# Encoder layer: the weight-block sums issued in the first group's middle phase, the down projection's residual by tiles, one of its steps later

## The chip, the cores and the metric

The kernel runs on one core of one Trainium2 chip. The metric is the device time of one execution in microseconds, as the median of several runs. A core has TensorE (PE, matmuls into PSUM), VectorE (DVE), ScalarE (ACT), GpSimd (POOL) and SyncE (SP), whose queue issues nearly all DMAs here. Each engine runs its own queue of instructions in order. PSUM holds matmul results, SBUF holds tiles, DRAM the inputs, outputs and scratch tensors.

## The reference

One layer of an encoder, run on two request groups of 1024 tokens by 1024 channels with the same weights, in fp32:

```
proj = x @ w_in                                     # mixers A and B side by side
oa   = rmsnorm(dilated window attention(qa, ka, va))
ob   = rmsnorm(grouped-query attention(qb, kb, vb))
x    = LN1(alpha*x + [oa, ob] @ w_o)
x    = LN2(alpha*x + softmax(x wc_q (mem wc_k)^T / 16) (mem wc_v) wc_o)   # 256 memory tokens, 4 heads
u    = x @ w_up;  gate, val = halves of u           # 2816 columns each
x    = LN3(alpha*x + (gelu(conv3(gate)) * val) @ w_down)
```

alpha is 2^(1/4), LN is a layer norm with gain and bias, conv3 a depthwise convolution of width 3 over the tokens.

## The kernel before, in words

The two groups (g = 0, 1) go through the same phases one after the other: phase_in (projection), attention, phase_mid (output projection, cross attention, two layer norms), ffn_up and ffn_down; cross_prep, for both groups at once, stands between phase_in and attention of g = 0. Every fp32 operand is split into a high half, rounded to the form that TensorE takes at full rate, and a low half (the rest), and each product is three matmuls: high by high, high by low, low by high. ACT or POOL makes the high half, DVE or POOL the low half (L115, L126).

phase_mid's output projection takes w_o in two column halves n. For each half four weight blocks are loaded into `raw` buffers and split into `wts` tiles (wload, L269), and the eight row tiles ct of 128 tokens follow. The cross attention does the same with the products G of queries and keys (L965 to L985) and U of values and output weights (L987 to L1017), which cross_prep made. In its last loop each row tile is standardized into a `raw` buffer, stored to yD, and transposed later by x2t.

Both FFN projections are done by a scheme with seven products in place of eight (Winograd's form of Strassen's): sums and differences of blocks of both operands, with the products added up in PSUM and in the sums behind it. ffn_up goes over 22 column blocks f. up_sums (L1023) loads two blocks of w_up into `raw` and lets POOL make three sums of them; up_weights (L1042) splits seven weight tiles; prod (L1091) multiplies; DVE adds the products up (L1105 to L1115), which frees PSUM banks; end (L1117) does the convolution, GELU and the product with val for the block before. For each pair of blocks, end makes the three sums of the activations (s1, s2, s4) and stores blocks and sums to hD and hS in DRAM.

down_sums (L1194) makes the matching sums of w_down: for each j of 11 it loads two row blocks of w_down into two `raw` buffers, lets POOL make four differences in place (L1203, L1204, L1206, L1207) and stores both buffers to wD in DRAM. It is called in ffn_up of g = 0 alone, after product 5 of each odd f (L1172); both groups' ffn_down read wD.

ffn_down does seven products m (in the order SEVEN, L1182), each over 11 steps k, on 128-row blocks: 77 steps of 12 matmuls. d_in (L1210) loads what a step needs, one activation block and one weight block, and splits them: ACT copies the high halves (L109), POOL and DVE subtract one half each (L1233). The first five steps are loaded alone into `raw`, the others by pairs into `wts`. Its calls run up to seven steps ahead of the matmuls. Step k = 10 reads hD[10], which the last end stores. y, the residual, is read from yD with two loads of 2 MB (L1243) into the two `res` buffers that hold ffn_up's working tiles; it is multiplied by LN2's gain and its bias is added (L1298, L1299), for tiles 0 to 3 in steps 2 to 5 of the first product and for tiles 4 to 7 in steps 2 to 5 of the second. evac (L1260) adds a product from PSUM to y, finish (L1272) does the last layer norm and stores the output.

The order on each engine is made by a planner at build time: it walks the program, takes the instruction that its own estimates call ready, earlier program text first, and hands out buffers as they fall free in its plan. An instruction written late can so be issued early. issue_after gives the planner an order without a wait on the chip. `raw` is one pool of three buffers of 4 KB a partition for the whole kernel; `wts` has six.

```
                    if i == 5 and g == 0 and f % 2:        # ffn_up, L1172
                        self.down_sums(f // 2, wD)
                if m < 2 and 2 <= k < 6:           # ffn_down, L1295
                    v = yt(4 * m + k - 2)
                    nc.vector.tensor_mul(v, v, gb[0])
                    nc.vector.tensor_add(v, v, gb[1])
```

Of the kernel before, what the change touches and what calls it, by code (L numbers as in the profile page):

```python
# [18 lines left out]
NT = 8  # L19
NMEM = 256  # L20
DFF = 2816
NFF = DFF // 128
# [49 lines left out]
class Trunk:  # L72
# [760 lines left out]
        nc.scalar.activation(out, y, AF.Identity, bias=rs[:, 1:2], scale=rs[:, 0:1])  # L833


    def phase_mid(self, g, S, o2s, ob, G, U, yD):
        nc, a = self.nc, self.a
        es = ExitStack()
        P = lambda name, bufs=1: es.enter_context(
# [7 lines left out]
        self.dma(gain, bcast_rows(a["out_norm_b"], 512))  # L847
        gb = self.ln_load(1)
        mT = []

        def m_t(ct):
            if ct >= NT - 2:
# [13 lines left out]
        for n in range(2):  # L866
            ns = slice(n * 512, n * 512 + 512)
            w = self.wload(lambda kp: w_o[:, 2 * kp:2 * kp + 2, ns], fast=0, after=self.sp_last)
            for ct in range(NT):
                xr = wtile("xr")  # L870
                nc.sync.dma_start(xr, x[ct * 128:(ct + 1) * 128, ns])
                if len(mT) < NT:
                    m_t(len(mT))
                p = self.pB()
                self.gemm(p, mT[ct], w)
                nc.vector.scalar_tensor_tensor(yt(ct)[:, ns], xr, ALPHA, p, op0=ALU.mult, op1=ALU.add)
                if n == 1:
# [87 lines left out]
        for n in range(2):  # L965
            w = self.wload(lambda kp: G[g][n, 2 * kp:2 * kp + 2].rearrange("k p c -> p k c"), fast=1)
            for ct in range(NT):
                if ct % 2 == 0:
                    pp = self.at_slot(2 + 4 * n + ct // 2, [128, 2, 2, 4, 128])
                    pT[n] += [pp[:, 0], pp[:, 1]]  # L970
                p = self.pB()
                self.gemm(p, x1T[ct], w)
                mn = self.small.tile([128, 2], F32, name="cmn")
                nc.vector.tensor_reduce(mn, p.rearrange("p (h k) -> p h k", h=2), axis=X, op=ALU.min)
                s = wtile()
                den = self.small.tile([128, 2], F32, name="cden")
# [18 lines left out]
        for n, ct in [(n, ct) for j in range(NT // 2) for n in range(2) for ct in (2 * j, 2 * j + 1)]:  # L995
            if n == 0:
                st[ct] = self.small.tile([128, 2, 6], F32, name="bst")
            if (n, ct) == (0, NT - 2):
                self.up_sums0()
            ns = slice(n * 512, n * 512 + 512)  # L1000
            p = self.pB()
            for k in range(8):
# [57 lines left out]
    def ffn_up(self, g, B, todo, hD, hS, wD):  # L1060
# [56 lines left out]
        def end(e, f):  # L1117
# [9 lines left out]
            if f % 2:  # L1127
# [2 lines left out]
                j, (d0, d1) = f // 2, ds  # L1130
                ds.clear()
                a11, a21, a12, a22 = d0[:, :512], d0[:, 512:], d1[:, :512], d1[:, 512:]
                s1, s2, s4 = sets[1][:, 3584:], sets[0][:, 3584:], e.u3
                nc.gpsimd.tensor_add(s1, a21, a22)
                nc.sync.dma_start(hD[j, 1], d1)
                nc.gpsimd.tensor_sub(a21, a11, a21)
# [15 lines left out]
        for f in range(NFF):  # L1152
            e = begin(f)
# [11 lines left out]
            else:  # L1165
                for i in ORDER:
# [2 lines left out]
                        end(*last)  # L1169
                    if i == 5 and f < NFF - 1:  # L1170
                        ready.append(weights(f + 1))
                    if i == 5 and g == 0 and f % 2:  # L1172
                        self.down_sums(f // 2, wD)
                    if f == NFF - 1 and i in (7, 5, 2, 4, 3):
                        self.d_in(g)
            last = (e, f)
# [8 lines left out]
    def down_src(self, hD, hS, wD):  # L1185
# [2 lines left out]
        hv, sv, tv = [t.rearrange("j i p c -> p j i c") for t in (hD, hS, wD)]  # L1188
        self.hsrc = {1: hv[:, :, 0, l], 2: hv[:, :, 1, l], 6: sv[:, :, 1], 5: sv[:, :, 0],
                     7: hv[:, :, 0, r], 3: sv[:, :, 2], 4: hv[:, :, 1, r]}  # L1190
        self.wsrc = {1: w[:, :, 0, l], 2: w[:, :, 1, l], 6: tv[:, :, 1, r], 5: tv[:, :, 0, l],
                     7: tv[:, :, 0, r], 3: w[:, :, 1, r], 4: tv[:, :, 1, l]}

    def down_sums(self, j, wD):  # L1194

        nc = self.nc
        r = []
        for o in range(2):
            t = self.raw.tile([128, D], F32, name="raw")
# [10 lines left out]
    def d_in(self, g):  # L1210

        nc = self.nc
        s = len(self.ds)
        m, k = divmod(s, self.NK)
        i = self.SEVEN[m]
        if not self.dr:

            n = 1 if s < 5 else min(2, self.NK - k)
            if s < 5:
                r = self.raw.tile([128, 1, 2, 512], F32, name="raw")  # L1220
            else:
# [14 lines left out]
    def ffn_down(self, g, yD, out):  # L1236
# [2 lines left out]
        self.lnp = es.enter_context(self.tc.tile_pool(name="lnp", bufs=1, side="right", reuse_waits="tile"))  # L1239
        gb = self.ln_load(2)  # L1240
        y = [self.resid.tile([128, 4, D], F32, name="res") for _ in range(2)]
        for i in range(2):
            nc.sync.dma_start(y[i], yD[4 * i:4 * i + 4].rearrange("c p d -> p c d"))  # L1243
        yt = lambda ct: y[ct // 4][:, ct % 4]
        pa = [self.pA() for _ in range(2)]
        sets = [[p[:, n * 512:n * 512 + 512] for p in pa for n in range(2)],
                [self.pT(), self.pO(), self.pT(), self.pO()]]
# [2 lines left out]
                3: (0, 1, False), 4: (1, 0, True)}  # L1250
        stats = {}

        def mm(p, m, k, q):
            i, t = self.SEVEN[m], self.ds[m * self.NK + k]
            c = slice(q * 128, q * 128 + 128)
            for x, l in ((0, 0), (0, 1), (1, 0)):
                nc.tensor.matmul(p, t[:, x, 0, c], t[:, l, 1], start=i in (1, 2, 5) and k + x + l == 0,  # L1257
                                 stop=k == self.NK - 1 and x == 1, skip_group_check=True)

        def evac(i, q, p):  # L1260
            th, n, first = goal[i]
# [14 lines left out]
        for m, i in enumerate(self.SEVEN):  # L1276
            bank = sets[m % 2]
            if i == 4:
                gb = self.ln_load(3)
                if g:  # L1280

                    while len(self.ds) < 7 * self.NK:
                        self.d_in(g)
                    for q in range(4):
                        for k in range(self.NK):
                            mm(bank[q], m, k, q)
                        finish(q)
                        evac(i, q, bank[q])
                        finish(4 + q)
                    break  # L1290
            for k in range(self.NK):
                s = m * self.NK + k
                while len(self.ds) < min(s + 7, 7 * self.NK):
                    self.d_in(g)
                if m < 2 and 2 <= k < 6:  # L1295

                    v = yt(4 * m + k - 2)
                    nc.vector.tensor_mul(v, v, gb[0])  # L1298
                    nc.vector.tensor_add(v, v, gb[1])  # L1299
                if i == 4 and k % 2 and k < 8:  # L1300
                    finish(k // 2)
                for q in range(4):
                    mm(bank[q], m, k, q)
# [8 lines left out]
    def run(self, stages=None):  # L1312
# [9 lines left out]
        for g in range(2):  # L1322
# [28 lines left out]
            with ExitStack() as es:  # L1351
                gemm_pools(es, 14)
                if "mid" in stages:
                    yD = dt(f"yD{g}", [NT, 128, D])
                    hD, hS = dt(f"hD{g}", [NFF // 2, 2, 128, T]), dt(f"hS{g}", [NFF // 2, 3, 128, 512])
                    B, todo = self.phase_mid(g, S, o2s, ob, G, U, yD)
# [43 lines left out]
```

## Time and profile before

| | us |
|---|---|
| median of 3 runs | 3297.7 (3297.68 to 3300.06) |
| the profiled execution, its own time | 3297.42 |
| its span, first to last instruction | 3295.6 |
| TensorE busy | 3124.1 (95%) |
| VectorE busy | 1929.7 (59%) |
| GpSimd busy | 1831.7 (56%) |
| ScalarE busy | 1325.8 (40%) |

The mean granted clock of TensorE is 0.973 of its 2.4 GHz. DMA moved 426.66 MB, a mean of 129 GB/s. A share of the span is an average over phases with different limits, so the rows further down are taken by phase. In order of time the phases of g = 0 end at about 217 us (phase_in), 405 (cross_prep), 735 (attention), 1030 (phase_mid), 1530 (ffn_up) and 1767 (ffn_down); those of g = 1 at about 1985, 2312, 2607, 3044 and 3295.

### The profile page before, as it was taken

Reading aid. Unit: us, or ns where it says so; the run is one execution under the profiler, and the core shown is the slowest. Engines: PE = TensorE matmul, PEld = TensorE weight load, DVE = VectorE, ACT = ScalarE, POOL = GpSimd, SP = SyncE. Lnnn points to the kernel's source line nnn. Section 1 sums busy time; section 2 is a strip of 40 time slices with the busy share of each in tenths; the row PEclk is TensorE's granted clock in tenths of the full one; section 3 lists DMA queues with packets and bytes.
Section 4 is the critical chain, followed back from the end, with each engine's and each line's share of the span. In section 5 each row is a group of like instructions: output and inputs, shape, how many; then the busy total and the mean of one; then the engine's idle time right before and its main releaser. Section 6 shows DMA issues by size and latency. Waiting matters only on the chain.

```text
span 3295.6 us, 43553 instructions
## 1 busy us (share of the span) xinstructions
PE 3124.1 (95%) x16161; PEld 2640.9 (80%) x16161; DVE 1929.7 (59%) x3135; ACT 1325.8 (40%) x2483; POOL 1831.7 (56%) x1317
## 2 busy tenths in 40 slices
PE   8999999999998999898899998999999999999798
PEld 6888899888887777776687888988888788888586
DVE  4152167884447666665637336688454676767745
ACT  2122167872434333232433116678233443333332
POOL 7373512883424767674767552178343376665665
PEclk9999999999999999999899999999999999999899
DMA  8445595003112434447754548600311233323861
GB/s 264 124 146 192 172 215 148 16 27 102 54 42 77 134 131 141 141 134 268 259 169 154 157 127 193 174 14 8 114 52 45 71 96 109 108 97 128 301 207 70
DMA packets 332649, 426.66 MB, mean 129 GB/s; under 512 B 21180, under 2 KB 214932, under 8 KB 331284
## 3 DMA queue, kind: packets, MB, share of 16 engines
q1 hardware_dynamic: 329844, 415.41, 40.2%
q10 hardware_dynamic: 2592, 8.46, 0.7%
q8 instruction: 127, 2.08, 0.3%
q14 instruction: 86, 0.70, 0.1%
HBM read 298.37 MB, written 129.63 MB: 130 GB/s over the span
## 4 chain that ended last, share of the span: by engine, by line
PE 72%; DMA 8%; POOL 7%; DVE 6%; issue 4%; ACT 2%; SPq 1%; POOLq 0%; ACTq 0%; DVEq 0%
PE pS L1096 6%; PE pO L132 5%; PE pO L130 5%; PE pO L131 5%; PE pT L132 5%; PE pT L130 5%; PE pT L131 5%; PE pS L1257 5%; PE pT L1096 4%; PE pO L1096 4%; PE pO L720 3%; PE pO L1257 3%; PE pT L1257 3%; PE pS L693 3%; PE pO L611 3%
## 5 line engine op out<-in xcount | busy, mean ns | idle before, releaser
L1096 PE MATMUL pS<-t,wts 128*128 128x512 f32 (+1 forms) x1656 | 399.4, 394 | 42.8 <-DVE res L1105 42.8
L126 POOL TENSOR_TENSOR wts<-raw,wts 128x512 fp32r<-128x512 f32 (+1 forms) x187 | 361.7, 1940 | 130.7 <-ACT wts L109 128.6
L1096 PEld LDWEIGHTS pS<-t,wts 128*128 128x128 f32 x1656 | 313.5, 197 | 113.0 <-DVE res L1105 51.0
L1233 POOL TENSOR_TENSOR t<-wts,t 128x512 fp32r<-128x512 f32 x144 | 264.6, 1850 | 141.6 <-ACT t L109 129.0
L1257 PE MATMUL pS<-t 128*128 128x512 f32 x1056 | 249.0, 396 | 43.2 <-ACT t L109 23.4
L1257 PEld LDWEIGHTS pS<-t 128*128 128x128 f32 x1056 | 201.6, 191 | 88.8 <-ACT t L109 24.2
L1096 PE MATMUL pT<-t,wts 128*128 128x512 f32 (+1 forms) x1104 | 262.1, 387 | 7.9 <-ACT t L109 5.9
L1096 PE MATMUL pO<-t,wts 128*128 128x512 f32 (+1 forms) x1104 | 259.1, 384 | 0.4 <-ACT t L109 0.4
L130 PE MATMUL pT<-wts,t 128*128 128x512 f32 (+1 forms) x640 | 250.1, 391 | 8.3 <-ACT wts L109 8.3
L130 PE MATMUL pO<-wts,t 128*128 128x512 f32 (+1 forms) x640 | 251.1, 392 | 3.7 <-ACT t L109 3.1
L109 ACT ACTIVATE t<-wts 128x1024 fp32r<-128x1024 f32 x144 | 150.8, 1058 | 252.2 <-PE pO L1257 85.0
L132 PE MATMUL pO<-wts,t 128*128 128x512 f32 (+1 forms) x640 | 248.4, 388 | 3.3 <-DVE t L115 1.7
L131 PE MATMUL pT<-wts,t 128*128 128x512 f32 (+1 forms) x640 | 247.5, 387 | 0.5 <-DVE wts L126 0.5
L131 PE MATMUL pO<-wts,t 128*128 128x512 f32 (+1 forms) x640 | 247.9, 388 | 0.0
L132 PE MATMUL pT<-wts,t 128*128 128x512 f32 (+1 forms) x640 | 247.6, 387 | 0.0
L1096 PEld LDWEIGHTS pT<-t,wts 128*128 128x128 f32 x1104 | 206.3, 194 | 49.8 <-ACT t L109 6.3
L1096 PEld LDWEIGHTS pO<-t,wts 128*128 128x128 f32 x1104 | 204.5, 192 | 40.4 <-ACT t L109 0.8
L1233 DVE TENSOR_TENSOR t<-wts,t 128x512 fp32r<-128x512 f32 x144 | 139.9, 990 | 137.8 <-ACT t L109 135.8
L696 DVE TENSOR_REDUCE mn<-pS 128x1 f32<-128x1024 f32 x128 | 155.9, 1218 | 37.4 <-PE pS L693 36.3
L125 POOL TENSOR_SCALAR ptb<-praw 128x512 fp32r<-128x512 f32 x116 | 75.6, 652 | 160.7 <-ACT praw L109 160.0
L720 PE MATMUL pO<-ptb,v 128*128 128x256 f32 x1024 | 164.5, 296 | 0.1
L126 DVE TENSOR_TENSOR wts<-xr,wts 128x512 fp32r<-128x512 f32 x86 | 98.0, 1140 | 105.9 <-ACT wts L109 104.9
(288 smaller groups left out, 7273.9 us busy)
## 6 DMA issues: line engine op xcount, KB each, us to landing
raw<-w_up SPq DMA_DIRECT2D x88, 512.0 KB, 3.9
hD<-d SPq DMA_DIRECT2D x44, 512.0 KB, 3.2
wts<-wD SPq DMA_DIRECT2D x40, 512.0 KB, 5.0
wts<-hD SPq DMA_DIRECT2D x36, 512.0 KB, 5.0
hS<-res SPq DMA_DIRECT2D x66, 256.0 KB, 2.6
raw<-w_in SPq DMA_DIRECT2D x32, 512.0 KB, 4.1
kst<-ka SPq DMA_DIRECT2D x32, 512.0 KB, 10.3
wts<-hS SPq DMA_DIRECT2D x30, 512.0 KB, 4.0
```

The lines of the kernel that those rows point to most:

```text
L109: self.nc.scalar.activation(out, in_, AF.Copy)
L126: return (nc.vector if dve else nc.gpsimd).tensor_sub(lo, raw, hi.bitcast(F32))
L130: mm(out, sh, mh, start=start, stop=False)
L131: mm(out, sh, ml, start=False, stop=False)
L132: mm(out, sl, mh, start=False, stop=stop)
L611: nc.tensor.matmul(po[:, n * 64:(n + 1) * 64], pt[:, n, j], v, start=j == 0, stop=j == 1)
L693: nc.tensor.matmul(p[:, ns], q[:, ct * 128:(ct + 1) * 128], ks[:, hl, ns], start=hl == 0, stop=hl == 1)
L696: nc.vector.tensor_reduce(mn, p, axis=X, op=ALU.min)
L720: nc.tensor.matmul(po[:, :256], bd["v"][:, k, h // 4], hl[l][:, k].rearrange("p a b -> p (a b)"), start=k == 0 and l == 0, stop=k == 7 and ...
L1096: nc.tensor.matmul(p, w[:, x, k], b[l][:, k, cs], start=i in (1, 6, 7, 5) and k + x + l == 0, stop=k == 3 and x == 1, skip_group_check=True)
L1233: e.tensor_sub(t[:, 1, x], r[:, x], t[:, 0, x].bitcast(F32))
L1257: nc.tensor.matmul(p, t[:, x, 0, c], t[:, l, 1], start=i in (1, 2, 5) and k + x + l == 0, stop=k == self.NK - 1 and x == 1, skip_group_che ...
```

## The change

- phase_mid takes wD and calls down_sums in g = 0 at eleven places: before row tiles 3 and 6 of each half of the output projection, before row tiles 2 and 5 of each half of the G products, and before row tiles 1, 3 and 4 of the first half of the U products. down_sums counts its own calls. ffn_up calls it no more.
- In end, for the last f, the sum s2 goes to the block's own u2 instead of the tail of the other `res` buffer.
- ffn_down's steps stand in a list. Step (0, 10), the last of the first product, comes after (1, 4). d_in loads two steps at once only where the next step in the list is the next k of the same product.
- y is loaded by tiles of 512 KB, the first four at the start and the other four at step 12. Its gain and bias are applied by residual, for tiles 0 to 3 in steps 10 to 13 (behind the step's matmuls) and for tiles 4 to 7 in steps 1, 3, 5 and 7 of the third product. The first product's banks are evacuated one by one in steps 16 to 19.

The core of the diff:

```diff
@@ phase_mid, output projection
             for ct in range(NT):
+                if g == 0 and ct in (3, 6):
+                    self.down_sums(wD)
@@ phase_mid, G products
+                if g == 0 and ct in (2, 5):
+                    self.down_sums(wD)
@@ phase_mid, U products
+            if g == 0 and n == 0 and ct in (1, 3, 4):
+                self.down_sums(wD)
@@ ffn_up, end
-                s1, s2, s4 = sets[1][:, 3584:], sets[0][:, 3584:], e.u3
+                s1, s2, s4 = sets[1][:, 3584:], sets[0][:, 3584:] if f < NFF - 1 else e.u2, e.u3
@@ ffn_up
-                    if i == 5 and g == 0 and f % 2:
-                        self.down_sums(f // 2, wD)
@@ down_src
+        self.steps = [(0, k) for k in range(10)] + [(1, k) for k in range(5)] + [(0, 10)]
+        self.steps += [(1, k) for k in range(5, 11)] + [(m, k) for m in range(2, 7) for k in range(self.NK)]
@@ d_in
-        m, k = divmod(s, self.NK)
+        m, k = self.steps[s]
...
-            n = 1 if s < 5 else min(2, self.NK - k)
+            n = 1 if s < 5 else 1 + ((m, k + 1) in self.steps[s + 1:s + 2])
@@ ffn_down
-        for i in range(2):
-            nc.sync.dma_start(y[i], yD[4 * i:4 * i + 4].rearrange("c p d -> p c d"))
+        for ct in range(4):
+            nc.sync.dma_start(yt(ct), yD[ct])
...
+        def residual(ct):
+            with self.tc.issue_after(self.mark.ins):
+                nc.vector.tensor_mul(yt(ct), yt(ct), gb[0])
+            nc.vector.tensor_add(yt(ct), yt(ct), gb[1])
...
+            if s == 12:
+                for ct in range(4, NT):
+                    nc.sync.dma_start(yt(ct), yD[ct])
+            if i == 4 and k % 2 and k < 8:
+                finish(k // 2)
+            for q in range(4):
+                mm(bank[q], s, q)
+            if 10 <= s < 14:
+                residual(s - 10)
+            if 16 <= s < 20:
+                evac(1, s - 16, sets[0][s - 16])
+            if i == 6 and k % 2 and k < 8:
+                residual(4 + k // 2)
+            if k == self.NK - 1 and m:
                 for q in range(4):
-                    mm(bank[q], m, k, q)
-            for q in range(4):
-                evac(i, q, bank[q])
+                    evac(i, q, bank[q])
```

mm is as before but takes the step's number s and keeps its last matmul in self.mark.

## Rows read from the trace of the kernel before

**Rows 1.** Busy by stage: start:end length, then PE, PEld, DVE, ACT, POOL, clock, DMA.

```profile
735.00:1026.00 291.00, 288.69 (x1395) 239.63 (x1394) 143.41 (x242) 96.58 (x183) 101.59 (x70) 1.00 0.20 68
1030.10:1529.50 499.40, 449.72 (x1952) 367.81 (x1951) 328.08 (x320) 170.05 (x263) 345.10 (x223) 0.95 0.42 141
...
2606.70:3044.30 437.60, 430.03 (x1955) 359.23 (x1955) 308.15 (x321) 172.94 (x264) 281.99 (x182) 0.98 0.33 107
```

**Rows 2.** TensorE's waits (total, times, longest): ffn_up g0, g1; phase_mid g0; ffn_down g1.

```profile
PE pS L1096 <- DVE res L1105: 42.1, 19, 5.0
...
PE pS L1096 <- DVE res L1105: 0.8, 1, 0.8
...
PE pS L265 <- DVE t L115: 1.9, 2, 1.0
...
PE pS L1257 <- ACT t L109: 10.6, 1, 10.6
PE pS L1257 <- POOL t L1233: 9.1, 1, 9.1
```

**Rows 3.** Waits in ffn_up: SP's and DVE's of g0, then DVE's of g1.

```profile
SPq L1029 <- DMA wD<-raw: 69.5, 19, 4.8
...
DVE wts L126 <- ACT wts L109: 103.6, 23, 9.2
...
DVE wts L126 <- ACT wts L109: 59.5, 34, 3.7
```

**Rows 4.** Timeline of PE: start, length, instruction, count, idle before and releaser.

```profile
1030.33 1.60 PE L1096 MATMUL pT<-t,wts 128*128 128x256 f32 x12
...
1529.51 24.19 PE L1257 MATMUL pS<-t 128*128 128x512 f32 x106
1566.46 1.22 PE L1257 MATMUL pS<-t 128*128 128x512 f32 x2 [12.76 <-ACT t L109]
...
1581.28 7.39 PE L1257 MATMUL pS<-t 128*128 128x512 f32 x21 [8.48 <-POOL t L1233]
...
1759.64 7.64 PE L1257 MATMUL pS<-t 128*128 128x512 f32 x33
...
2606.97 1.59 PE L1096 MATMUL pT<-t,wts 128*128 128x256 f32 x12
...
3044.28 23.73 PE L1257 MATMUL pS<-t 128*128 128x512 f32 x104
3078.66 1.22 PE L1257 MATMUL pS<-t 128*128 128x512 f32 x2 [10.64 <-ACT t L109]
...
3273.08 7.78 PE L1257 MATMUL pS<-t 128*128 128x512 f32 x33 [0.78 <-DVE res L1265]
```

**Rows 5.** Timelines of SP, DVE and POOL at the entry to ffn_down of g0.

```profile
1543.45 0.32 SPq L1137 DMA_DIRECT2D hD<-d  x1
...
1545.18 0.57 SPq L1243 DMA_DIRECT2D res<-yD  x1
...
1557.64 4.63 DVE L1298 TENSOR_TENSOR res<-res,lng 128x1024 f32<-128x1024 f32 x4 [13.67 <-DMA lng<-ln_g]
...
1566.48 14.74 POOL L1233 TENSOR_TENSOR t<-wts,t 128x512 fp32r<-128x512 f32 x1 [23.06 <-ACT t L109]
```

**Rows 6.** Chain of waits in order of time: start, length, what.

```profile
1548.34 16.99 DMA wts<-hD
...
1617.68 29.92 PE pS L1257 x132
```

**Rows 7.** down_sums' POOL operations, first and last of four: ns min/median/max, starts.

```profile
L1203 POOL TENSOR_TENSOR raw<-raw x11: 1297/1735/1754, 1070.3 to 1500.9; 128x512 f32<-128x512 f32 x11
...
L1207 POOL TENSOR_TENSOR raw<-raw x11: 1288/1293/1635, 1082.2 to 1511.4; 128x512 f32<-128x512 f32 x11
```

**Rows 8.** The page's DMA issues: line, queue, count, KB each, median us to landing.

```profile
raw<-w_down SPq DMA_DIRECT2D x22, 512.0 KB, 3.6
wD<-raw SPq DMA_DIRECT2D x22, 512.0 KB, 4.7
```

**Rows 9.** Timeline of POOL in phase_mid of g0.

```profile
788.62 1.05 POOL L125 TENSOR_SCALAR wts<-raw 128x1024 fp32r<-128x1024 f32 x1 [39.05 <-PE pT L132]
```

More of the change, by code (lines that the diff above doesn't have):

```diff
@@ L833, in standardize, with phase_mid @@
         nc.scalar.activation(out, y, AF.Identity, bias=rs[:, 1:2], scale=rs[:, 0:1])
-    def phase_mid(self, g, S, o2s, ob, G, U, yD):
+    def phase_mid(self, g, S, o2s, ob, G, U, yD, wD):
         nc, a = self.nc, self.a
@@ L849, in phase_mid @@
         mT = []
+        self.nsums = 0
         def m_t(ct):
@@ L1190, in down_src, with down_sums @@
                      7: hv[:, :, 0, r], 3: sv[:, :, 2], 4: hv[:, :, 1, r]}
+        self.steps = [(0, k) for k in range(10)] + [(1, k) for k in range(5)] + [(0, 10)]
+        self.steps += [(1, k) for k in range(5, 11)] + [(m, k) for m in range(2, 7) for k in range(self.NK)]
         self.wsrc = {1: w[:, :, 0, l], 2: w[:, :, 1, l], 6: tv[:, :, 1, r], 5: tv[:, :, 0, l],
                      7: tv[:, :, 0, r], 3: w[:, :, 1, r], 4: tv[:, :, 1, l]}
-    def down_sums(self, j, wD):
-        nc = self.nc
+    def down_sums(self, wD):
+        nc, j = self.nc, self.nsums
+        if j == self.NK:
+            return
+        self.nsums += 1
         r = []
@@ L1251, in ffn_down, with mm @@
         stats = {}
-        def mm(p, m, k, q):
-            i, t = self.SEVEN[m], self.ds[m * self.NK + k]
-            c = slice(q * 128, q * 128 + 128)
+        def mm(p, s, q):
+            (m, k), t = self.steps[s], self.ds[s]
+            i, c = self.SEVEN[m], slice(q * 128, q * 128 + 128)
             for x, l in ((0, 0), (0, 1), (1, 0)):
-                nc.tensor.matmul(p, t[:, x, 0, c], t[:, l, 1], start=i in (1, 2, 5) and k + x + l == 0,
-                                 stop=k == self.NK - 1 and x == 1, skip_group_check=True)
+                self.mark = nc.tensor.matmul(p, t[:, x, 0, c], t[:, l, 1], start=i in (1, 2, 5) and k + x + l == 0,
+                                             stop=k == self.NK - 1 and x == 1, skip_group_check=True)
         def evac(i, q, p):
@@ L1274, in finish @@
             nc.scalar.dma_start(out[ct * 128:(ct + 1) * 128], yt(ct))
-        for m, i in enumerate(self.SEVEN):
-            bank = sets[m % 2]
-            if i == 4:
+        def residual(ct):
+            with self.tc.issue_after(self.mark.ins):
+                nc.vector.tensor_mul(yt(ct), yt(ct), gb[0])
+            nc.vector.tensor_add(yt(ct), yt(ct), gb[1])
+        N = len(self.steps)
+        for s, (m, k) in enumerate(self.steps):
+            i, bank = self.SEVEN[m], sets[m % 2]
+            if i == 4 and k == 0:
                 gb = self.ln_load(3)
                 if g:
-                    while len(self.ds) < 7 * self.NK:
+                    while len(self.ds) < N:
                         self.d_in(g)
                     for q in range(4):
-                        for k in range(self.NK):
-                            mm(bank[q], m, k, q)
+                        for t in range(s, N):
+                            mm(bank[q], t, q)
                         finish(q)
@@ L1290, in ffn_down @@
                     break
[L1291 to L1301, printed above, removed]
+            while len(self.ds) < min(s + 7, N):
+                self.d_in(g)
+            if s == 12:
[12 more added lines that the diff above has]
+            if k == self.NK - 1 and m:
                 for q in range(4):
-                    mm(bank[q], m, k, q)
-            for q in range(4):
-                evac(i, q, bank[q])
+                    evac(i, q, bank[q])
         if not g:
@@ L1355, in run @@
                     hD, hS = dt(f"hD{g}", [NFF // 2, 2, 128, T]), dt(f"hS{g}", [NFF // 2, 3, 128, 512])
-                    B, todo = self.phase_mid(g, S, o2s, ob, G, U, yD)
+                    B, todo = self.phase_mid(g, S, o2s, ob, G, U, yD, wD)
                 if "ffn" in stages:
```

## The prediction

> **What bounds the kernel now.** I read the busy table by stage first. In the FFN up projection of the first request group TensorE is busy 449.72 of 499.40 us; in the same code for the second group it is busy 430.03 of 437.60 [rows 1]. The one thing that the first group does and the second doesn't is the eleven calls of down_sums. TensorE's waits agree: 42.1 us in 19 waits on the DVE add of L1105 in the first group, 0.8 us in the second [rows 2]. L1105 is late because DVE, which runs in order, stands behind the low halves of the next weights (L126): 103.6 us of waiting there in the first group, 59.5 in the second. The next weights are late because their load waits for a `raw` buffer: 69.5 us in 19 waits of w_up loads on the store of wD out of such a buffer [rows 3]. So one shared pool of three buffers, not POOL's busy time, is what the moved step costs.
>
> The second place is the entry to ffn_down, in both groups. TensorE runs nine steps without a pause (106 matmuls in 24.19 us), then stands 12.76 us for the ACT copy of step 9 and 8.48 us for POOL's half of the same split [rows 4]; the second group shows 10.6 and 9.1 us [rows 2]. Steps 9 and 10 are loaded as one pair, and step 10 reads the last hD, stored at 1543.45; the pair, issued after a yD load of 2 MB (1545.18), needed 16.99 us to land. Then POOL's one subtraction lasted 14.74 us, while DVE ran the residual's multiplies and adds back to back (four of them 4.63 us, 1.16 each; 16 in all) [rows 5, 6]. Elsewhere TensorE goes from matmul to matmul in 29.92/132 = 0.2267 us [rows 6].
>
> **The change part by part.** The profiled execution took 3297.42 us, its span 3295.6, so 1.8 us lie around it; the median of the runs is 3297.7. I sum against 3297.4.
>
> (a) down_sums leaves ffn_up. With the same code and no down_sums, the second group takes from 2606.97 to 3044.28, 437.31 us, against 1030.33 to 1529.51, 499.18 us [rows 4]. Of the nine steps' 108 matmuls that follow, two stand before the end of the first stretch and four before that of the second (106 and 104 are left), 0.45 us apart. The gain is 499.18 - 437.31 + 0.45 = 62.3 us. It holds the 42 us of waits and the slower matmuls after each of them: the granted clock was 0.95 of 2.4 GHz there and 0.98 in the second group [rows 1]. The least it can be is the waits' difference, 42.1 - 0.8 = 41.3; I take 62.3, because the second group is the nearer row.
>
> (b) down_sums arrives in phase_mid of the first group. Per call: two loads, four POOL operations of 1.29 to 1.74 us, two stores. POOL gets 345.10 - 281.99 = 63.1 us in all and would be busy 101.59 + 63.1 = 165 of 291 us; the 23 MB add 79 GB/s to 68, together 147, about the 141 that ffn_up carried [rows 1, 7, 8]. TensorE waits 1.9 us there now, on nothing of POOL's [rows 2], and POOL has a hole of 39.05 us before it splits a block of the second w_o half, for which it waits on TensorE and not on data [rows 9]. Behind the new SP loads stand, on SP, the x rows and the loads of w_o, G and U; behind the new POOL operations stand the weight splits and the one-column powers of the norms, for which ACT and then the transposes wait. Bounds: -2 (the 1.9 us can only shrink) and 11 x 62.3/11 = 62 us, the price that a call has in ffn_up. I take 5, a few late powers in the cross attention's output loop, where three calls share `raw` with the standardized rows.
>
> (c) Step 9 is loaded alone, and step 10, with the last hD, goes behind five steps of the next product. From 1529.51, 24.19 us for the nine steps and six more steps of 12 x 0.2267 = 2.72 us put its first matmul at 1570.0; with the load no faster than now its first half was split by 1566.46 [rows 4]. In the second group the same sum gives 3084.3 against 3078.66. So the DMA waits of 12.76 and 10.6 us go, with 3.5 and 5.7 us in hand, and the load now has less traffic ahead of it: y comes by tiles, the first four as soon as the up projection's first buffer is free (the last s2 no longer sits in it), the other four at step 12. What is late next is the landing of the LayerNorm rows, for which DVE waited 13.67 us [rows 5]; nothing but the residual needs them.
>
> (d) The residual's multiplies and adds go one tile a step (steps 10 to 13) and one tile every second step of the third product; the evacuation of the first product is spread over four steps. The same 16 multiplies and adds remain. DVE gets 2.3 us of residual and its half of a split in a step of 2.72, so over four steps it is at its limit, with steps in hand. POOL's wait of 8.48 and 9.1 us should go, with the slow clock that follows each stall.
>
> The two entries together, by their ends: from 1529.51 to 1767.28 is 237.8 us for 922 matmuls that need 209.0, and from 3044.28 to 3280.86 is 236.6 for 920 that need 208.5 [rows 4, 6]. That is 28.8 and 28.1 us over. I leave 3 us of each in place, for DVE and POOL meeting in steps 10 to 13, so the gain is 25.8 + 25.1 = 50.9. Bounds: nothing but the two DMA waits (23.4) and the whole 56.9.
>
> On that meeting rows and notes differ. The row: one POOL subtraction stayed open for 14.74 us across some dozen DVE operations [rows 5]. The Trainium skill, SBUF — State Buffer, section Who interferes with whom, says that a DVE instruction with two SBUF inputs contends with a GpSimd instruction that reads SBUF, and that the one which issues first has the shared pair for that whole instruction. By that rule POOL would lose one DVE instruction at a time, 1.16 us, and the sum would be up to 6 us lower, 3183, which lies in the forecast's own range. By the row it loses the whole of an unbroken DVE run, and how unbroken the new run is decides.
>
> **Sum.** 3297.4 - 62.3 + 5 - 50.9 = 3189.2 us.
>
> **The rivals.**
> Residual still starves POOL. The mark that spreads it is a matmul, while the operations are DVE's; if the order planned for DVE still puts several tiles together, DVE runs 8 operations of 1.16 us in a row just before step 15 and POOL's halves come late again. For it stands the 14.74 us [rows 5]. Against: the splits of up to six steps are already made when the run begins. Then the POOL waits stay (8.48 + 9.1) and about half of the slow clock around them (5): 3189.2 - 6 + 22.6 = 3206.
>
> The price moves with the calls. Three `raw` buffers feed w_o, G, U and the standardized rows as they fed w_up; if a call costs in phase_mid what it cost in ffn_up, 5.7 us, the first gain is gone: 3189.2 - 5 + 62.3 = 3246. For it: the same pool [rows 3] and a store of 4.7 us at the end of each call [rows 8]. Against: TensorE's weights there last for eight row tiles, not for one pass, and lie ready early [rows 9].
>
> Slower. In phase_mid each call puts itself between TensorE and its next weight block for as long as it holds a `raw` buffer: 3.6 us of load, three POOL operations (3.9 to 5.2 us, say 4.2) and 4.7 us of store [rows 7, 8], 12.5 us. Eleven of these are 137.5 us: 3297.4 - 62.3 - 50.9 + 137.5 = 3322. It decides from (62.3 + 50.9)/11 = 10.3 us a call. Against: POOL's 39.05 us hole [rows 9].
>
> Nothing gained. The entry's waits stay and the calls cost their old price, so that the work has only changed places: 3297.
>
> **How the numbers follow.** The forecast, 62 in 100; the starved POOL 17, the moved price 12, slower 5, no change 4. The range of 8 in 10 goes from 3176 (the sum with all of both entries gone and 2 us gained in phase_mid: 3297.4 - 62.3 - 56.9 - 2) to 3235, which takes in the starved POOL with a phase_mid cost of up to 34 us, and leaves out most of the moved price. A measurement of this kernel tells about 0.2%, 6.6 us, from no change. Faster is the first three cases, 91 in 100; within that, 4; slower, 5.
>
> **What would show it.** The stretch of ffn_up in the first group should take about 437 us, with no wait on L1105 beyond 1 us or so, and w_up loads that no longer wait on a wD store. In ffn_down's entry there should be no TensorE wait over 3 us, step 9 should run straight after step 8, and POOL's subtraction should never last 10 us. Phase_mid of the first group should stay within 5 us or so of the second's 291. The prediction is wrong if phase_mid grows by over 30 us, if TensorE waits on POOL's L1233 again, or if ffn_up's waits stay without down_sums.

## The result and the profile after

The changed kernel takes 3223.7 us (median of 4 runs, 3220.9 to 3231.1) against 3297.8 before: a ratio of 0.9777, 95% interval 0.9759 to 0.9795. That is faster and inside the range, but 35 us above the forecast of 3189. The profiled execution took 3221.8 us, its span 3219.8 against 3295.6; the 75.8 us between the spans are accounted for by stage below.

The lines of the change have moved: the up projection's matmul is now L1103 and its add L1112, the down projection's matmul L1268, its split half L1244, its evacuation L1276, the residual's multiply L1290 and add L1291. The busy table by stage of the changed kernel (start:end length, PE, PEld, DVE, ACT, POOL, clock, DMA share, GB/s) for phase_mid, ffn_up and the whole of ffn_down of the first group, then ffn_up of the second; it answers to [rows 1].

```profile
735.00:1026.00 291.00, 286.65 (x1374) 236.87 (x1373) 145.64 (x240) 94.80 (x181) 156.50 (x113) 1.00 0.42 147
1030.60:1467.90 437.30, 429.23 (x1954) 358.36 (x1953) 308.18 (x321) 175.37 (x267) 283.80 (x182) 0.98 0.35 116
1467.90:1699.50 231.60, 213.85 (x921) 175.36 (x919) 136.06 (x146) 77.78 (x74) 146.11 (x84) 0.96 0.58 201
2543.90:2980.30 436.40, 427.03 (x1954) 356.67 (x1953) 306.70 (x320) 172.11 (x263) 279.33 (x180) 0.99 0.35 113
```

The first group's ffn_up has become the second's: 437 us, clock 0.98. POOL's 55 us more (156.50 for 101.59) and the traffic (147 GB/s for 68) have arrived in phase_mid.

TensorE's waits after (total, times, longest), answering to [rows 2]: ffn_up of the first group, phase_mid of the first group, then ffn_down of the first and of the second.

```profile
PE pS L932 <- ACT raw L833: 3.2, 1, 3.2
...
PE pS L265 <- DVE bmv L807: 1.7, 1, 1.7
...
PE pS L1268 <- DVE t L1244: 12.2, 1, 12.2
PE pT L1268 <- DVE t L1244: 4.1, 1, 4.1
...
PE pT L1268 <- DVE t L1244: 9.2, 2, 7.8
PE pS L1268 <- DVE res L1276: 3.2, 3, 1.8
```

The 42.1 us on the add have gone. Phase_mid waits 2 us more, on small vectors of a norm. In ffn_down the long waits for ACT and POOL have gone (one of 1.4 us for ACT is left in the first group), and waits for DVE's half of a split stand in their place.

The waits of SP and DVE in the first group's ffn_up, answering to [rows 3]: no w_up load waits for a wD store any more, and DVE's wait for the high halves fell from 103.6 to 68.9 us.

```profile
SPq L1036 <- POOL wts L126: 263.7, 38, 15.3
...
DVE wts L126 <- ACT wts L109: 68.9, 39, 3.8
```

Two readings of [rows 3] need care. Its second DVE row, 59.5 us, covers 2650 to 3000 us alone; over the whole stage the second group waited 67.6 us there, in 38 waits, and the first group now waits about as long. And the waits of the w_up loads are not a price: on POOL's splits alone they total 263.7 us now (83.0 us before, beside the 69.5 on the stores), and TensorE's 42.1 us have gone all the same.

TensorE's timeline after (start, length, instruction, count, idle before and releaser), answering to [rows 4]: the first group's entry, the second group's first matmul of ffn_up and the second entry. Behind the 116 matmuls of the first row stand 62 more without a wait, up to 1508.35, most of them of the second product.

```profile
1467.85 26.46 PE L1268 MATMUL pS<-t 128*128 128x512 f32 x116
...
1523.19 4.26 PE L1268 MATMUL pS<-t 128*128 128x512 f32 x10 [12.19 <-DVE t L1244]
...
2543.87 1.60 PE L1103 MATMUL pT<-t,wts 128*128 128x256 f32 x12
...
2980.29 26.80 PE L1268 MATMUL pS<-t 128*128 128x512 f32 x116
```

By stage: up to ffn_up +0.3 us (1030.62 for 1030.33); the first ffn_up 437.2 for 499.2, -62.0; the first ffn_down 231.6 for 237.8, -6.2; from there to the second ffn_up 844.4 for 839.7, +4.7; the second ffn_up -0.9; the second ffn_down 225.4 for 236.6, -11.2; the end -0.6. Together -75.8.

How the entry looks inside. DVE, POOL and SP of the changed kernel, first group (same columns; a row's count is of like instructions in a run):

```profile
1485.49 1.77 DVE L1145 TENSOR_TENSOR res<-res,d 128x512 f32<-128x512 f32 x1
1487.19 1.77 DVE L1244 TENSOR_TENSOR t<-wts,t 128x512 fp32r<-128x512 f32 x1
1488.89 1.77 DVE L1146 TENSOR_TENSOR res<-d,res 128x512 f32<-128x512 f32 x1
1503.54 13.50 DVE L1290 TENSOR_TENSOR res<-res,lng 128x1024 f32<-128x1024 f32 x8 [12.88 <-DMA lng<-ln_g]
1516.96 4.50 DVE L1291 TENSOR_TENSOR res<-res,lnb 128x1024 f32<-128x1024 f32 x2
1521.39 1.74 DVE L1244 TENSOR_TENSOR t<-wts,t 128x512 fp32r<-128x512 f32 x1
...
1483.27 1.75 POOL L1141 TENSOR_TENSOR res<-d 128x512 f32<-128x512 f32 x1
1484.98 1.74 POOL L1244 TENSOR_TENSOR t<-wts,t 128x512 fp32r<-128x512 f32 x1
1486.68 1.73 POOL L1143 TENSOR_TENSOR d<-d 128x512 f32<-128x512 f32 x1
...
1491.10 0.38 SPq L1144 DMA_DIRECT2D hD<-d  x1
1492.88 1.74 SPq L1313 DMA_DIRECT2D res<-yD  x4
1494.67 0.45 SPq L794 DMA_DIRECT2D lng<-ln_g  x1
...
1495.91 1.29 SPq L1235 DMA_DIRECT2D wts<-hD  x2
```

Two things are to be seen. First, all eight multiplies of the residual, for both halves of y, stand in one run on DVE ahead of the next split half (1503.54 to 1521.39); TensorE waits for that half from 1511.00 to 1523.19. Four of the eight are marked behind matmuls of the third product, which TensorE starts only at 1549.69: the marks held nothing back. Second, split halves now stand among the last block's own sums (L1141 and L1143 on POOL, L1145 and L1146 on DVE), so that the last hD is stored at 1491.10, 23.3 us after the stretch began, where it was 13.9 us before (1543.45 - 1529.51, [rows 4, 5]); the second four tiles of y, the LayerNorm rows and the next loads stand behind that store on SP.

The chain of waits of the changed kernel (start, length, what) goes through the same pieces in the second group:

```profile
2992.91 3.98 POOL t L1244 x2
...
2999.26 1.30 POOL res L1141
3000.63 1.81 POOL d L1143
3002.45 2.62 DMA hD<-d
3005.10 3.94 DMA lng<-ln_g
...
3019.80 4.54 DVE res L1291 x2
3024.34 1.80 DVE t L1244 x3
```

Split halves, then the late sums, the hD store, the LayerNorm rows, the residual, and a split half behind it.

### The profile page after: what moved, and what is told of

Its sections match the earlier page's. It is cut to its first block, busy times and chain, and to the rows that moved or that the text cites. A ratio compares the mean times of both kernels' runs of the same rounds, so it can differ in the third digit from the quotient of the medians.

```text
span 3219.8 us, 43612 instructions
## 1 busy us (share of the span) xinstructions
PE 3096.5 (96%) x16161; PEld 2624.8 (82%) x16161; DVE 1935.0 (60%) x3135; ACT 1324.4 (41%) x2483; POOL 1808.8 (56%) x1317
## 5 line engine op out<-in xcount | busy, mean ns | idle before, releaser
L1103 PE MATMUL pS<-t,wts 128*128 128x512 f32 (+1 forms) x1656 | 379.0, 382 | 0.8 <-DVE res L1112 0.8
L1103 PEld LDWEIGHTS pS<-t,wts 128*128 128x128 f32 x1656 | 304.4, 190 | 60.3 <-DVE res L1112 1.3
L1244 POOL TENSOR_TENSOR t<-wts,t 128x512 fp32r<-128x512 f32 x144 | 250.2, 1748 | 146.7 <-ACT t L109 135.3
L1103 PE MATMUL pT<-t,wts 128*128 128x512 f32 (+1 forms) x1104 | 259.8, 384 | 10.2 <-ACT t L109 5.9
L1268 PE MATMUL pS<-t 128*128 128x512 f32 x1056 | 244.6, 391 | 15.4 <-DVE t L1244 12.2
L1103 PE MATMUL pO<-t,wts 128*128 128x512 f32 (+1 forms) x1104 | 257.1, 382 | 0.2 <-ACT t L109 0.2
L1268 PEld LDWEIGHTS pS<-t 128*128 128x128 f32 x1056 | 199.1, 189 | 58.9 <-DVE t L1244 12.6
L1103 PEld LDWEIGHTS pT<-t,wts 128*128 128x128 f32 x1104 | 204.0, 192 | 51.1 <-ACT t L109 6.3
L1103 PEld LDWEIGHTS pO<-t,wts 128*128 128x128 f32 x1104 | 202.9, 190 | 40.2 <-ACT t L109 0.7
L1244 DVE TENSOR_TENSOR t<-wts,t 128x512 fp32r<-128x512 f32 x144 | 141.6, 1002 | 119.7 <-ACT t L109 119.7
```

The lines of the kernel that those rows point to most:

```text
L1103: nc.tensor.matmul(p, w[:, x, k], b[l][:, k, cs], start=i in (1, 6, 7, 5) and k + x + l == 0, stop=k == 3 and x == 1, skip_group_check=True)
L1244: e.tensor_sub(t[:, 1, x], r[:, x], t[:, 0, x].bitcast(F32))
L1268: self.mark = nc.tensor.matmul(p, t[:, x, 0, c], t[:, l, 1], start=i in (1, 2, 5) and k + x + l == 0, stop=k == self.NK - 1 and x == 1, sk ...
```

## The experiments

Times are medians of timed runs, or one run where that is said; ratios are to the kernel before, run on the same chip.

**The marks.** The changed kernel, with the residual's multiply and add each held behind DVE's newest split half instead of the multiply alone behind a matmul:

```diff
-            with self.tc.issue_after(self.mark.ins):
+            with self.tc.issue_after(self.half.ins):   # half: the split's last subtraction, on DVE
                 nc.vector.tensor_mul(yt(ct), yt(ct), gb[0])
-            nc.vector.tensor_add(yt(ct), yt(ct), gb[1])
+                nc.vector.tensor_add(yt(ct), yt(ct), gb[1])
```

> The changed kernel with one edit: residual's multiply and add are ordered behind DVE's half of the newest split (the same queue) and no longer behind a matmul. Theory (DVE's in-order queue: eight multiplies and two adds, planned together, wait for the LayerNorm rows and then stand ahead of the split halves of steps 15 and on): the DVE waits of 12.2 + 4.1 us in the first group's entry and 9.2 us in the second's go, with their slow clock; ffn_down takes 231.6 and 225.4 us in the changed kernel and should take 211 to 215 in each, and the whole 3221.8 - 28 = 3194 us, 3188 to 3200. Rival (the late hD and the traffic of the y loads set the entry, DVE is only the last in line): 3215 to 3225, the waits stand under ACT's copies instead. Rival (POOL starves whenever DVE does residual work, however it is spread): 3205 to 3215, waits on POOL's halves.

Measured: 3207.0 us, 0.9733 [0.9718, 0.9747]; the entries 226.8 and 217.9 us. The bunch is gone and about 15 us with it, less than the 3188 to 3200 that I expected. The time lies where the rival of the starved POOL had it, but its wait is not there: POOL's halves are awaited 0.4 us. TensorE's waits left in the first entry are 6.4 us for DVE's halves and 5.5 for an evacuation behind them. DVE of this kernel now alternates, but it begins late, after 16 us of waiting for ACT's part of a split whose load stands on SP behind the late hD store:

```profile
1504.04 0.69 DVE L1244 TENSOR_TENSOR t<-wts,t 128x512 fp32r<-128x512 f32 x1 [16.05 <-ACT t L109]
...
1508.03 2.31 DVE L1290 TENSOR_TENSOR res<-res,lng 128x1024 f32<-128x1024 f32 x1
1510.26 1.78 DVE L1244 TENSOR_TENSOR t<-wts,t 128x512 fp32r<-128x512 f32 x1
```

**The floor.** The changed kernel without the residual's 16 multiplies and adds (the output lacks that norm's gain and bias):

```diff
-            with self.tc.issue_after(self.mark.ins):
-                nc.vector.tensor_mul(yt(ct), yt(ct), gb[0])
-            nc.vector.tensor_add(yt(ct), yt(ct), gb[1])
```

> The changed kernel without residual's sixteen multiplies and adds in each ffn_down (gain and bias of the second layer norm are left out of the residual). Theory: with nothing of residual on DVE the entries have no wait over 2 us and the time is the floor for any order of them, 3185 to 3195. Rival (hD and DMA traffic): 3210 to 3225.

Measured: 3187.0 us (one run). The first ffn_down of this kernel, in the columns of the busy table, runs at full clock; the second takes 209.8 us:

```profile
1472.30:1681.70 209.40, 209.03 (x921) 172.44 (x919) 118.50 (x130) 77.46 (x74) 142.58 (x84) 1.00 0.62 222
```

Everything that is left in the changed entries, 22 and 16 us, goes through these 16 operations; but leaving them out hides whether they are too many, too bunched or too late.

**The moved sums alone.** The kernel before, with only down_sums moved into phase_mid:

```diff
-                    if i == 5 and g == 0 and f % 2:
-                        self.down_sums(f // 2, wD)
+                if g == 0 and ct in (3, 6):      # output projection
+                    self.down_sums(wD)
+                if g == 0 and ct in (2, 5):      # cross attention's output loop
+                    self.down_sums(wD)
+            if g == 0 and n == 0 and ct in (1, 3, 4):
+                self.down_sums(wD)
```

> The kernel before with only down_sums moved to phase_mid, ffn_down as it was. Theory: the move is worth 62 us by itself and costs phase_mid under 1 us: 3297.7 - 62 = 3236, 3231 to 3241, ffn_up of the first group 437 us, and the entries keep their ACT waits of 12.8 and 10.6 and POOL waits of 8.5 and 9.1 us. Rival (part of the gain in ffn_up was from the other edits): 3245 to 3280.

Measured: 3238.1 us, 0.9824 [0.9810, 0.9838]; the first ffn_up 437.0 us, phase_mid unchanged. So some 58 us are this part's alone. Both entries stay as they were (237.1 and 237.3 us), with the old waits; the first group's for ACT, of this kernel:

```profile
PE pS L1265 <- ACT t L109: 11.7, 1, 11.7
```

**The order of the steps.** e1_behind_split with step 10 back in its natural place, loaded as a pair with step 9:

```diff
-        self.steps = [(0, k) for k in range(10)] + [(1, k) for k in range(5)] + [(0, 10)]
-        self.steps += [(1, k) for k in range(5, 11)] + [(m, k) for m in range(2, 7) for k in range(self.NK)]
+        self.steps = [(m, k) for m in range(7) for k in range(self.NK)]
```

> The first kernel of this set (residual behind the split halves) with the steps in their natural order again, so that steps 9 and 10 are loaded as one pair and the last hD is needed at step 10. Theory: the wait for that pair is real and comes back under ACT's copy, some 5 to 13 us in each group plus slow clock, 3200 to 3222. Rival (the wait was made by the 4 MB of y ahead of the pair, and y by tiles takes it away without the reordering): 3190 to 3198, as with the steps reordered.

Measured: 3199.4 us (one run), the entries 215.3 and 216.3. The pair, which TensorE awaited for 12.76 and 10.64 us before [rows 4], is awaited for 2.2 and 1.0; the first group's row here:

```profile
PE pS L1267 <- ACT t L109: 2.2, 1, 2.2
```

So it was mainly the y traffic ahead of it that had made the pair late: the pair's first load took 16.99 us to land before [rows 6] and takes 7.0 us here, behind y by tiles. The last hD is stored 11.9 us after the stretch began, not 23. With these marks the reordering cost more than it gave.

**Natural order with the change's own marks.** The changed kernel with the same one edit of self.steps:

> The changed kernel with only the order of the steps undone (step 10 of the first product in its place, mark behind the matmul as in the change). Theory (the reordering lets the split halves of steps 9 to 14 go ahead of the last block's sums on DVE and POOL, so that the last hD is stored 23 us after the up projection's end and not 12, and eight multiplies can gather behind it): faster than the changed kernel, 3205 to 3214, last hD stored 12 us after the end, the multiplies in a group of four instead of eight. Rival (the reordering hides the wait for the last hD as meant, and undoing it brings that wait back): 3230 to 3245.

Measured: 3218.8 us, 0.9769 [0.9747, 0.9790], which can't be told from the changed kernel; the entries 227.0 and 227.8 us. Neither my 3205 to 3214 nor the rival's 3230 to 3245 was met. The pair is awaited 2.3 and 1.2 us, and DVE of this kernel shows the bunch again, four in a run, behind the landing of the LayerNorm rows:

```profile
1497.88 4.63 DVE L1289 TENSOR_TENSOR res<-res,lng 128x1024 f32<-128x1024 f32 x4 [9.33 <-DMA lng<-ln_g]
```

**A wider spread.** e5_natural_steps with the residual at steps 11, 13, 15 and 17, and the evacuation two steps later:

```diff
-            if 10 <= s < 14:
-                residual(s - 10)
-            if 16 <= s < 20:
-                evac(1, s - 16, sets[0][s - 16])
+            if s in (11, 13, 15, 17):
+                residual((s - 11) // 2)
+            if 18 <= s < 22:
+                evac(1, s - 18, sets[0][s - 18])
```

> Steps in natural order, residual behind the split halves, and wider: tiles 0 to 3 in steps 11, 13, 15 and 17, the first product's banks evacuated in steps 18 to 21. Theory (after the pair with the last hD the splits have no lead, and DVE needs some steps without residual to win it back): the remaining wait of 4.6 us on DVE's halves goes, ffn_down 211 to 214 us in each group against 215.3 and 216.3 with steps 10 to 13, and the whole 3190 to 3196. Rival (the wait for the pair and the slow clock behind it are all that is left): 3197 to 3201, no change. Rival (the evacuation comes too late for the third product, which needs the same banks): 3203 or more, with waits on evac.

Measured: 3211.4 us, 0.9750 [0.9735, 0.9764], slower than without it. The third product starts at step 22 in the banks that the evacuation empties, and TensorE now waits for it there; the second group:

```profile
PE pS L1267 <- DVE res L1275: 10.7, 2, 9.9
```

**The last block's sums first.** e1_behind_split, with the split halves from step 9 on held behind the last block's own sums, on POOL and on DVE; first one run, then timed:

```diff
+                self.endp = nc.gpsimd.tensor_sub(a21, a11, a21)
...
+                self.endv = nc.vector.tensor_sub(s4, a12, s2)
...
+            with self.tc.issue_after((self.endp, self.endv)[x].ins) if s > 8 else ExitStack():
                 self.half = e.tensor_sub(t[:, 1, x], r[:, x], t[:, 0, x].bitcast(F32))
```

> Reordered steps and residual behind the split halves, and the split halves of steps 9 and later ordered behind the last block's own sums on DVE and POOL. Theory (the lateness of the last hD is what the reordering costs): last hD stored 12 to 14 us after the up projection's end, ffn_down 213 to 218 us where it was 226.8 and 217.9, the whole 3193 to 3201. Rival (the cost is in the loads of step 15 and on, behind 3 MB of y and LayerNorm rows, whenever the hD is stored): 3204 to 3210.

> The kernel of e8_sums_first again, timed. If its 3185.09 was representative: 3182 to 3189, ratio to the kernel before 0.965 to 0.967, both entries at 209 to 211 us. If that one look was lucky by as much as the runs of the changed kernel spread (3220.9 to 3231.1): up to 3195.

Measured: 3185.1 (one run), then 3187.1 us, 0.9672 [0.9652, 0.9691]: faster than both kernels, and than the 3193 to 3201 that I first expected. SP, POOL and DVE of the timed one, in the first group: the hD store is 10 us earlier (13.1 us after 1465.13), the rows of LayerNorm follow it at 1483, POOL and DVE share the halves behind the sums, and DVE reaches the residual at 1494.71, 13 us earlier than in e1_behind_split. The second four tiles of y are loaded behind the next blocks here (1486.90), and ahead of them in e1_behind_split (1490.22 before 1493.34); that came with the hold, and what it is worth by itself was not tried.

```profile
1478.23 0.32 SPq L1144 DMA_DIRECT2D hD<-d  x1
...
1482.99 0.33 SPq L794 DMA_DIRECT2D lng<-ln_g  x1
...
1476.41 1.80 POOL L1143 TENSOR_TENSOR d<-d 128x512 f32<-128x512 f32 x1
1478.17 10.21 POOL L1245 TENSOR_TENSOR t<-wts,t 128x512 fp32r<-128x512 f32 x6
...
1478.68 10.25 DVE L1245 TENSOR_TENSOR t<-wts,t 128x512 fp32r<-128x512 f32 x6
...
1494.71 2.32 DVE L1291 TENSOR_TENSOR res<-res,lng 128x1024 f32<-128x1024 f32 x1
```

The entry of this kernel, in the columns of the busy table: nothing is left above the floor.

```profile
1465.10:1673.90 208.80, 208.73 (x921) 172.49 (x919) 145.46 (x146) 77.56 (x74) 153.24 (x84) 1.00 0.64 222
```

**The same hold with the marks of the change, and with the natural order.** Two edits of e8_sums_first, one at a time:

```diff
-            with self.tc.issue_after(self.half.ins):
+            with self.tc.issue_after(self.mark.ins):
                 nc.vector.tensor_mul(yt(ct), yt(ct), gb[0])
-                nc.vector.tensor_add(yt(ct), yt(ct), gb[1])
+            nc.vector.tensor_add(yt(ct), yt(ct), gb[1])
```

> The changed kernel with the residual's marks as they are (behind a matmul) and only the split halves held behind the last block's sums. Theory: the bunch of residual operations on DVE and the late hD cost separately, so the hold gives the 22 us that it gave between e1_behind_split (3207) and e8_sums_first (3185), and a wait of several us for a DVE half stays in each entry: 3199 to 3206. Rival: the bunch only hurts because the halves behind it come late; once hD is early the splits are done before it and its cost is gone: 3184 to 3190.

```diff
-        self.steps = [(0, k) for k in range(10)] + [(1, k) for k in range(5)] + [(0, 10)]
-        self.steps += [(1, k) for k in range(5, 11)] + [(m, k) for m in range(2, 7) for k in range(self.NK)]
+        self.steps = [(m, k) for m in range(7) for k in range(self.NK)]
```

> e8_sums_first with step 10 back in its natural place, loaded as one pair with step 9. Theory: the reordering earns nothing by itself, because the pair's load was late only for the y traffic and the late hD; then a wait of 1 to 2 us for the pair in each entry, 3186 to 3191. Rival: with the sums first the reordering does what it was made for, and without it the pair's wait of some 10 us returns in each entry: 3200 to 3207.

Measured: 3204.0 us, 0.9723 [0.9706, 0.9739], for the change's own marks with the hold; DVE's half is still awaited, 5.9 us in the first entry and 11.1 in the second. With e10's marks and hold and the natural order 3199.3, 0.9711 [0.9697, 0.9726]. So the marks and the hold work side by side: from 0.9777, the marks alone give 0.44 points, the hold alone 0.54, both 1.05. And the reordering does pay, 12 us, once the sums come first: my 3186 to 3191 was wrong. The rival's time, 3200 to 3207, is nearly met, but not by its cause. The pair is awaited 1.9 and 0.3 us, not 10; TensorE waits 3.5 us for DVE's halves in each entry instead, and the entries take 216.2 and 215.6 us for 208.7 and 210.2. In the natural order the hold itself gives nothing (3199.3 here, 3199.4 in e5_natural_steps), since the last hD is early there anyway.

**What down_sums cost in ffn_up.** The kernel before without POOL's four subtractions, and the kernel before with the two stores copying rows of w_down within DRAM, so that no store holds a `raw` buffer (the differences are missing from both outputs):

```diff
-        nc.gpsimd.tensor_sub(b11, b12, b11)
-        nc.gpsimd.tensor_sub(b12, b22, b12)
...
-        nc.gpsimd.tensor_sub(b22, b22, b11)
-        nc.gpsimd.tensor_sub(b21, b21, b22)
```

> The kernel before without the four POOL differences of down_sums in ffn_up (wD gets the plain weight blocks). Theory (the price of a call is that two of three raw buffers are held from the load to the end of the store): ffn_up of the first group keeps a third to two thirds of its 62 us over the second's 437, 455 to 480 us, with w_up loads still waiting for wD stores. Rival (the price is POOL's 63 us of added work): 437 to 442 us.

```diff
-        nc.sync.dma_start(wD[j, 0], r[0])
+        nc.sync.dma_start(wD[j, 0], self.a["w_down"][0][(2 * j + 0) * 128:(2 * j + 1) * 128])
...
-        nc.sync.dma_start(wD[j, 1], r[1])
+        nc.sync.dma_start(wD[j, 1], self.a["w_down"][0][(2 * j + 1) * 128:(2 * j + 2) * 128])
```

> The kernel before with the two wD stores of each down_sums copying the rows of w_down in DRAM instead of the differences, so that no store holds a raw buffer; loads, POOL's four subtractions and the bytes written stay (the differences are left out of the output). The prediction's mechanism (a store of 4.7 us holds one of the three raw buffers, the w_up load behind it comes late): most of the 62 us goes, the first group's ffn_up at 437 to 450 us, 3236 to 3250. Rival (POOL runs in order, and four more operations that wait for their own load stand between it and the splits): ffn_up stays at 480 to 499 us, 3279 to 3298.

Measured: 3242.1 and 3308.0 us (one run each). The first group's ffn_up in the busy table, without the subtractions and then without the stores (the kernels that keep down_sums out of this stage took 436.2 to 439.2 us in it):

```profile
1030.20:1471.70 441.50, 429.53 (x1953) 355.88 (x1952) 305.80 (x319) 169.40 (x264) 275.94 (x180) 0.99 0.50 161
```

```profile
1058.90:1538.30 479.40, 441.23 (x1953) 361.42 (x1951) 322.37 (x319) 172.06 (x263) 349.46 (x224) 0.97 0.39 125
```

Of 61.9 us, 57.7 go with POOL's work, though loads, stores and traffic stay; without the stores 42.1 remain. The second kernel's whole time says nothing: with nothing to wait for, its copies were all issued at the start, where they made the way to ffn_up 28.5 us longer (1058.86 for 1030.33). The row of the first store of each call, eleven of them (ns min/median/max, first and last start):

```profile
L1205 SPq DMA_DIRECT2D wD<-w_down x11: 488/488/637, 15.1 to 51.1; - x11
```

They also took their 11.5 MB out of ffn_up, so the 19.7 us that they give back are the store's hold of the buffer and its traffic together, an upper bound for the hold. Leaving out the subtractions also lets a buffer go sooner, so the two gains overlap (57.7 and 19.7 are more than 61.9). How they hang together stands in the chain of waits of the kernel before, here for one call:

```profile
1251.95 3.10 DMA raw<-w_down
1255.19 1.39 POOL raw L1204
1256.65 1.64 POOL raw L1206
1258.36 0.91 POOL raw L1207
1259.27 4.56 DMA raw<-w_up
```

Nine of the eleven calls stand on that chain. In six of them it goes as here from POOL's last subtraction straight to the next load of w_up, and in three through a store of wD. In the second group's ffn_up the chain runs through TensorE instead.

## Why the prediction was right in sign and wrong in size

**(a) Right: 62.0 us measured for 62.3.** The second group was a true copy of the first without the step. But half of the cause named for the price fell: I wrote that the pool of three buffers, not POOL's busy time, is what the step costs. The four subtractions' 64.9 us of POOL work (18.0, 17.8, 14.6 and 14.5) cost 57.7; with pool, loads and stores still there, but no subtractions, 4.2 us of the price are left. The pool passes POOL's delay on: the chain above goes from a subtraction to the next w_up load, and from there to POOL's next sums and splits. The store, on which I had read the price, is on it in three of those nine calls.

**(b) Right in kind: 0.3 us measured for 5.** Neither the moved price nor the slower case came: 55 us of work went into POOL's idle time in phase_mid.

**(c) Half right.** TensorE runs 178 matmuls at the first entry without a pause where it ran 106, and the 12.76 and 10.64 us for ACT are gone. Three things were missed. Y by tiles would have done most of it without the reordering (2.3 and 1.2 us are left in e7_changed_natural_steps). "Nothing but the residual needs them" was true of the LayerNorm rows, but DVE runs in order and what stands behind the residual waits too. And the new order let split halves get in among the last block's sums and delayed the very hD that it was to give time; "with the load no faster than now" took its store as fixed. Holding the halves back gave 0.54 points, some 18 us, and only then was the reordering worth its 12.

**(d) The term that was mis-sized.** The gain of both entries together was 50.9 in the sum and 17.4 in the run (6.2 and 11.2). I left 3 us of each; 22.6 and 16.9 stayed. The step that failed is that the multiplies go "one tile a step". The mark was a matmul, and DVE's planned order put eight multiplies in one run (in the first group; four in the second). That was the first rival's mechanism, with its sign right and its victim wrong: POOL was not starved (its longest half took 2.3 us, not 14.74), DVE's own half stood behind the run. The 14.74 us against which the prediction weighed this meeting did not come back; DVE paid instead. I had priced a multiply or add at 1.16 us, and beside POOL they took 2.3, so that the run of eight multiplies and two adds lasted 17.9 us. The rival's price, 3206, was too low for that reason and because the late hD came on top. With both mended, the time is 3187, by the forecast's path: the entries at their floor, 209 and 210 us.

**What was luck.** The profiled run lies 32.6 us above the sum, and 33.5 of that are this term. The rest agrees by luck: the 4.7 us too many in (b) and the 4.7 us of the stretch below cancel. That the time fell inside the range is partly luck too, since its upper part was argued from a starved POOL and a dearer phase_mid, and neither came.

**Open.** From the first ffn_down's end to the second ffn_up the changed kernel needs 4.7 us more. In the other kernels that stretch took 839.0 to 845.9 us, 839.0 in e7_changed_natural_steps, which has all of the change but the reordering. With the sums moved alone it took 842.9. Its cause is open; single profiles of kernels that do the same work there differ by up to 7 us, so it may be no more than that.

## What to carry to other kernels

Put the mark that spreads work on the engine that does the work: here DVE operations marked behind matmuls were still planned in one run ahead of the split halves, and marked behind DVE's own halves they alternated. When a late input is given more time by reordering, look at what the steps pulled forward do to the engine that makes that input; here they delayed it by 10 us. A second pass over the same code without the moved step sizes its removal well, but not why it cost: that took leaving out its parts one by one, and the chain of waits. A large total in the table of waits is not yet a price: the loads of w_up wait longer after the change than before it.

## What was not expected of the hardware

DVE operations with two SBUF inputs that started while a POOL subtraction ran took 1.10 us more, at both sizes seen: 0.68 became 1.78 for 512 columns and 1.21 became 2.31 for 1024 (the rows of e1_behind_split show both sizes beside POOL). In the changed kernel all 20 residual operations that started so took 2.28 to 2.32 us, and the other 12 took 1.21 to 1.23. Six halves on POOL and six on DVE side by side took 10.21 and 10.25 us, 1.70 each, somewhat less than one after the other would take (0.68 + 1.29 = 1.97). That agrees with the Trainium skill, SBUF — State Buffer, section Who interferes with whom, that a two-input DVE instruction contends with a GpSimd instruction reading SBUF. No such delay of DVE was seen at the entry before, where DVE's operations went on at 1.16 us and one POOL subtraction stayed open for 14.74 us [rows 5]. What decides between the two was not tried.
